# Expert numbers in a product-key retrieval: comparisons and products in float16, choices innermost, on VectorE

## The chip, the cores and the metric

The kernel runs on one core of a Trainium2 chip. The core has TensorE (PE, matrix products; PEld is its loading of weights), VectorE (DVE), ScalarE (ACT), GpSimd (POOL) and SyncE (SP, which here issues DMAs). The metric is the device time of one execution in microseconds (us); the time quoted is the median of several executions. Beside them stands one execution taken with the profiler, from which all rows below come.

## The reference

A decoder block for 512 tokens of 1024 channels: RMS norm, a mixer (RWKV-7 heads and sliding-window attention), an output product, and a channel mixer `peer_ffn` that fetches experts. Only the last is touched. Cut to what matters:

```python
def block(x_b):                                   # 128 tokens; H = 8 heads, K = 16
    q = (x_b @ wq).reshape(-1, H, 2, PEER_HALF)
    s = jnp.einsum('thcd,hcnd->thcn', q, subkeys)         # 128 scores for each half c
    s_top, i_top = lax.top_k(s, K)
    cand_s = (s_top[:, :, 0, :, None] + s_top[:, :, 1, None, :]).reshape(-1, H, K * K)
    cand_i = (i_top[:, :, 0, :, None] * PEER_N_KEYS + i_top[:, :, 1, None, :]).reshape(-1, H, K * K)
    best_s, best_pos = lax.top_k(cand_s, K)
    idx = jnp.take_along_axis(cand_i, best_pos, axis=-1).reshape(-1, H * K)
    gate = jax.nn.softmax(best_s, axis=-1).reshape(-1, H * K)
    u = u_tab[idx]
    act = jax.nn.gelu(jnp.einsum('td,ted->te', x_b, u), approximate=False)
    return jnp.einsum('te,ted->td', gate * act, v_tab[idx])
```

So for each token and head the 16 best keys of either half are found, their sums are ranked again, and the 16 winners give 16 expert numbers (first key x 128 + second key) with gates.

## The kernel before

Stages, in the time of the profiled execution: the mixer and the output product up to about 390 us; the choice of experts from there to about 600 us, which is where the change lies; a stage of one-hot products that lays the gates out over all experts (605 to about 820 us); and then products of all 128 blocks of experts with `u` and `v` on TensorE to the end. One token tile of the four goes through gathered rows instead (`gather`, on POOL's DMA queue).

**The choice.** The loop over `hc` (16 steps: 8 heads x 2 halves) splits a block of `wq` into high and low part (`wq_split`: `wqh` cast on ScalarE L165, `wql` subtracted on POOL L166), makes the query with 24 matmuls (`pq`), and the scores with four (`psc`, copied to `sc`). `top` (L926) then picks the 16 best of 128 scores on VectorE for the four token tiles: two MAX8, two index searches and one replacement per row, L929 to L937. After every four steps two heads are complete, which makes eight rows of 16 + 16 keys, `tv` values and `ti` numbers.

`choose(h0, tv, ti)` (L939) works on such a group of two heads. It is a generator that is advanced twice in each later step of the loop, so that a group's work lies among the next four steps; the last group (`h0` = 6) runs behind the loop. Up to the first stop: `fi`, the key numbers as float32; `df`, the differences of neighbouring numbers (L945, and an addition for the first half L946); and `cand`, the 50 sums that can be among the best 16 (nine instructions L951 and L953). `E_` is POOL for the first three groups and VectorE for the last. Then `top` on the candidates gives `bv` and `bp`, the positions 0 to 49. `ex` (L966) is the exponent's argument; ScalarE takes its exponential (L969 for the last group, L1005 otherwise).

`pick` (L976) turns positions into numbers without a gather. For each position it compares with 15 thresholds (`ge`, L981, four rows at once: 4 x 16 x 15 = 960 elements, two instructions, on VectorE), multiplies the 0/1 result with the differences (L987, two instructions, on `E_`), and sums (L992) and adds the first number (L993, VectorE). The first `pick` gives first key and place in the list (`offs` holds the thresholds, packed with the number by 128s), the second the second key (thresholds `iota`). Results go to `sg_`, the table of gates and key numbers that all later stages read.

**What runs beside it.** TensorE fills the time with products of `uT` blocks that belong to the later expert stage (`up_steps`, L896). For each of a list of 64 blocks: `up_load` on SyncE (four buffers `u`), `up_split` (`uh` cast on ScalarE L165; `ul` subtracted, L166, on POOL for block numbers 1 to 19 and on VectorE otherwise; two buffers each), `up_product` (24 matmuls of 384 columns in two steps, lines L175 to L177 in turn, each `ul` read by L177), and `up_act` (gelu on ScalarE, L888). The split of the next block is issued one block ahead. `UPS1` and `UPST` say how many half products follow each `hc` step (0, 1, 0, 0, then 2 each) and each stop of the last group (3 each). P14, P16, P17 and P18 in the text are products number 14, 16, 17 and 18 of that list, counted from 0.

The order on every engine is that in which the code is written (`manual_schedule`), the generators' interleaving included; an engine runs its list strictly in that order and waits at the front of it. All buffers of `choose` exist twice.

Of the kernel before, what the change touches and what calls it, by code (L numbers as in the profile page):

```python
# [7 lines left out]
F32 = mybir.dt.float32  # L8
F32R = mybir.dt.float32r
HF = mybir.dt.float16  # L10
# [3 lines left out]
OP = mybir.AluOpType  # L14
AX = mybir.AxisListType
# [7 lines left out]
TOPK = 16  # L23
# [31 lines left out]
OFFS = [sum(NCAND[:a]) for a in range(16)]  # L55
# [20 lines left out]
def _emit(ctx, tc, A, out, dbg, stop):  # L76
    nc = tc.nc
    V, SC, PE, GP, SY = nc.vector, nc.scalar, nc.tensor, nc.gpsimd, nc.sync
# [56 lines left out]
    for lv in range(5):  # L135
        b = 1 << lv
        n = 32 // (2 * b)
        for q in range(4):
# [5 lines left out]
                             pattern=[[-2 * b, n], [0, b]], compare_op=OP.is_ge, fill=0.0,  # L144
                             base=0, channel_multiplier=1)
# [621 lines left out]
    mpst, mp = right("mp")  # L767
# [3 lines left out]
    SY.dma_start(ln2r, A["ln2r"])  # L771
    iota = mp.tile([128, 128], F32, name="iota")
    GP.iota(iota, pattern=[[1, 128]], base=0, channel_multiplier=0, allow_small_or_imprecise_dtypes=True)

# [144 lines left out]

    offs = tk.tile([128, 2, 15], F32, name="offs")  # L920
    for a in range(1, 16):
        GP.memset(offs[:, 0, a - 1:a], float(OFFS[a]))
        GP.memset(offs[:, 1, a - 1:a], 128.0 * (OFFS[a] - OFFS[a - 1]))
    B815 = [128, 4, TOPK, 15]

# [13 lines left out]
    def choose(h0, tv, ti):  # L939

        E_ = GP if h0 < 6 else V
        fi = tk.tile([128, 2, 8, TOPK], F32, name="fi", tag="fi", bufs=2)
        V.tensor_copy(fi, ti)
        df = tk.tile([128, 2, 8, 15], F32, name="df", tag="df", bufs=2)
        E_.tensor_tensor(out=df, in0=fi[:, :, :, 1:16], in1=fi[:, :, :, 0:15], op=OP.subtract)  # L945
        E_.tensor_tensor(out=df[:, 0], in0=df[:, 0], in1=offs[:, 1, None, :].to_broadcast([128, 8, 15]), op=OP.add)  # L946
        cand = tk.tile([128, 8, NC_], F32, name="cand", tag="cand", bufs=2)
# [20 lines left out]
        if h0 == 6:  # L968
            SC.activation(ex, ex, AF.Exp)  # L969
        pf = tk.tile([128, 8, TOPK], F32, name="pf", tag="pf", bufs=2)  # L970
        V.tensor_copy(pf, bp)
        ro = tk.tile([128, 8, TOPK], F32, name="ro", tag="ro", bufs=2)
        rn = tk.tile([128, 8, TOPK], U32, name="rn", tag="rn", bufs=2)

        def pick(src, steps, base, dst):

            ges = []
            for hh in range(2):
                hs = slice(4 * hh, 4 * hh + 4)
                ge = tk.tile(B815, F32, name="ge", tag="ge", bufs=2)  # L980
                V.tensor_tensor(out=ge, in0=src[:, hs, :, None].to_broadcast(B815),  # L981
                                in1=steps[:, None, None, :].to_broadcast(B815), op=OP.is_ge)
                ges.append(ge)
            yield
            for hh in range(2):
                hs = slice(4 * hh, 4 * hh + 4)
                E_.tensor_tensor(out=ges[hh], in0=ges[hh],  # L987
                                                    in1=df[:, base, hs, None, :].to_broadcast(B815), op=OP.mult)
            yield
            for hh in range(2):  # L990
                hs = slice(4 * hh, 4 * hh + 4)
                V.tensor_reduce(dst(hh), ges[hh], axis=AX.X, op=OP.add)  # L992
                V.tensor_tensor(out=dst(hh), in0=dst(hh), in1=fi[:, base, hs, 0:1].to_broadcast([128, 4, TOPK]),  # L993
                                op=OP.add)


        yield from pick(pf, offs[:, 0, :], 0, lambda hh: ro[:, 4 * hh:4 * hh + 4])
        V.tensor_copy(bp, ro)
# [3 lines left out]
        V.tensor_tensor(out=pf, in0=pf, in1=ro, op=OP.subtract)  # L1002
        yield from pick(pf, iota[:, 1:16], 1, lambda hh: sg_[:, 2, :, h0 + hh, :])
        if h0 < 6:
# [394 lines left out]
```

## Time and profile before

| | us |
|---|---|
| median of 3 runs | 1654.14 |
| lowest, highest | 1652.88, 1655.71 |
| profiled execution, its time | 1651.63 |
| its span in the trace | 1649.9 |
| TensorE busy, of the span | 1584.4 (96%) |
| VectorE busy | 1279.5 (78%) |
| POOL busy | 712.3 (43%) |
| ScalarE busy | 655.2 (40%) |

The mean granted clock of TensorE is 0.992 of full speed. Busy shares are averages over stages that have different limits, so for the change only the stretch of the choice counts, about 430 to 600 us, and what waits there. In that stretch TensorE has matmuls to do nearly all the time, VectorE is full too, and POOL serves both: TensorE with `wql` and `ul`, VectorE with candidates and the products L987. The last chain of the page runs mostly over TensorE (49%), then VectorE (11%).

In rows of the timeline the first number is the start, the second the duration; in brackets stands how long the engine was idle before it and what released it.

### The profile page before, as it was taken

Reading aid. Unit: us, or ns where it says so; the run is one execution under the profiler, and the core shown is the slowest. Engines: PE = TensorE matmul, PEld = TensorE weight load, DVE = VectorE, ACT = ScalarE, POOL = GpSimd, SP = SyncE. Lnnn points to the kernel's source line nnn. Section 1 sums busy time; section 2 is a strip of 40 time slices with the busy share of each in tenths; the row PEclk is TensorE's granted clock in tenths of the full one; section 3 lists DMA queues with packets and bytes.
Section 4 is the critical chain, followed back from the end, with each engine's and each line's share of the span. In section 5 each row is a group of like instructions: output and inputs, shape, how many; then the busy total and the mean of one; then the engine's idle time right before and its main releaser. Section 6 shows DMA issues by size and latency. Waiting matters only on the chain.

```text
span 1649.9 us, 30181 instructions
## 1 busy us (share of the span) xinstructions
PE 1584.4 (96%) x11629; PEld 1362.9 (83%) x11629; DVE 1279.5 (78%) x2474; ACT 655.2 (40%) x1078; POOL 712.3 (43%) x670
## 2 busy tenths in 40 slices
PE   5999999898999989999999999999999999999997
PEld 4777677676898889888888888888888888888886
DVE  5656548745799989999868778877878877787797
ACT  5444345534343435445433333333333333333334
POOL 5112110033577612222235555555565655556582
PEclk9999999999999999999999999999999999999999
DMA  4111120141222249998999988988988989889794
GB/s 135 53 41 41 53 60 2 58 166 52 90 103 91 78 162 318 331 360 316 337 325 354 330 308 298 332 311 304 341 304 310 319 310 325 306 289 352 244 305 147
DMA packets 180113, 369.57 MB, mean 224 GB/s; under 512 B 17792, under 2 KB 102272, under 8 KB 179712
## 3 DMA queue, kind: packets, MB, share of 16 engines
q1 hardware_dynamic: 137056, 225.14, 40.0%
q0 software_dynamic: 36864, 134.23, 22.4%
q10 hardware_dynamic: 6048, 8.26, 1.4%
q8 instruction: 91, 1.49, 0.4%
q14 instruction: 54, 0.44, 0.1%
HBM read 332.04 MB, written 35.52 MB: 223 GB/s over the span
## 4 chain that ended last, share of the span: by engine, by line
PE 49%; DVE 11%; DMA 3%; issue 2%; ACT 1%; SPq 0%; POOL 0%; DVEq 0%; POOLq 0%; ACTq 0%
PE acc L1271 10%; PE acc L1269 10%; PE acc L1270 10%; PE pA L177 7%; PE pA L175 7%; PE pA L176 7%; DVE O L1140 3%; DVE ul L166 2%; DVE scr L1094 2%; DVE P L1145 2%; DMA u<-in_uT_dram 1%; DMA row<-in_vB_dram,ix 0%; DMA gts<-gates 0%; DMA acts<-actd 0%; PE pG L1167 0%
## 5 line engine op out<-in xcount | busy, mean ns | idle before, releaser
L177 PE MATMUL pA<-h2hi,ul 128*128 128x384 f32 x1024 | 348.3, 340 | 10.2 <-DVE ul L166 6.1
L175 PE MATMUL pA<-h2hi,uh 128*128 128x384 f32 x1024 | 354.0, 346 | 3.0 <-ACT uh L165 1.6
L176 PE MATMUL pA<-h2lo,uh 128*128 128x384 f32 x1024 | 346.4, 338 | 0.0
L1271 PE MATMUL acc<-vl,wh 128*128 128x512 f32 x768 | 299.1, 389 | 1.1 <-DVE vl L166 1.1
L1269 PE MATMUL acc<-vh,wh 128*128 128x512 f32 x768 | 299.5, 390 | 0.6 <-ACT vh L165 0.6
L1270 PE MATMUL acc<-vh,wl 128*128 128x512 f32 x768 | 299.3, 390 | 0.0
L1081 POOL DMA_INDIRECT row<-in_u_dram,ix x128 | 175.6, 1372 | 284.8 <-DVE scr L1094 246.5
L1081 POOL DMA_INDIRECT row<-in_vB_dram,ix x128 | 195.9, 1530 | 142.5 <-DVE x L1092 118.9
L166 DVE TENSOR_TENSOR vl<-v,vh 128x1024 fp32r<-128x1024 f32 x128 | 217.1, 1697 | 35.9 <-ACT vh L165 35.0
L177 PEld LDWEIGHTS pA<-h2hi,ul 128*128 128x128 f32 x1024 | 193.3, 189 | 15.3 <-DVE ul L166 11.2
L175 PEld LDWEIGHTS pA<-h2hi,uh 128*128 128x128 f32 x1024 | 193.4, 189 | 6.8 <-ACT uh L165 2.1
L176 PEld LDWEIGHTS pA<-h2lo,uh 128*128 128x128 f32 x1024 | 193.4, 189 | 3.0
L1092 DVE SCALAR_TENSOR_TENSOR x<-row,ac,x 128x1024 f32<-128x1024 f32 x128 | 172.6, 1348 | 6.0 <-DMA row<-in_vB_dram,ix 4.2
L1271 PEld LDWEIGHTS acc<-vl,wh 128*128 128x128 f32 x768 | 144.2, 188 | 32.6 <-DVE vl L166 2.1
L1269 PEld LDWEIGHTS acc<-vh,wh 128*128 128x128 f32 x768 | 144.2, 188 | 28.5 <-ACT vh L165 0.9
L1270 PEld LDWEIGHTS acc<-vh,wl 128*128 128x128 f32 x768 | 144.1, 188 | 27.4
L1094 DVE SCALAR_TENSOR_TENSOR scr<-row,h2g 128x1024 f32<-128x1024 f32 x128 | 158.8, 1240 | 1.5 <-DMA row<-in_u_dram,ix 0.2
L165 ACT CAST uh<-u 128x1024 fp32r<-128x1024 f32 x128 | 133.9, 1047 | 61.3 <-PE pA L176 33.0
L166 DVE TENSOR_TENSOR ul<-u,uh 128x1024 fp32r<-128x1024 f32 x109 | 134.8, 1238 | 21.2 <-ACT uh L165 20.9
L165 ACT CAST vh<-v 128x1024 fp32r<-128x1024 f32 x128 | 134.0, 1047 | 0.1
L1168 ACT ACTIVATE gst<-pG 128x512 f32<-128x512 f32 x96 | 55.9, 597 | 100.6 <-PE pG L1167 98.8
L888 ACT ACTIVATE act<-pA 128x384 f32<-128x384 f32 x86 | 42.2, 491 | 132.6 <-PE pA L177 132.6
(711 smaller groups left out, 2508.0 us busy)
## 6 DMA issues: line engine op xcount, KB each, us to landing
u<-in_uT_dram SPq DMA_DIRECT2D x128, 512.0 KB, 8.1
v<-in_vB_dram SPq DMA_DIRECT2D x128, 512.0 KB, 6.3
gts<-gates SPq DMA_DIRECT2D x384, 64.0 KB, 5.1
gates<-gst SPq DMA_DIRECT2D x11, 2048.0 KB, 11.8
w<-in_w_in_dram SPq DMA_DIRECT2D x40, 256.0 KB, 3.2
wq<-in_wq_dram SPq DMA_DIRECT2D x16, 512.0 KB, 3.5
acts<-actd ACTq DMA_DIRECT2D x42, 192.0 KB, 6.1
act<-acts SPq DMA_DIRECT2D x42, 192.0 KB
```

What stands on the lines that cost most here:

```text
L165: (hi_eng or SC.copy)(dst_hi, src)
L166: (lo_eng or V).tensor_tensor(out=dst_lo, in0=src, in1=dst_hi.bitcast(F32), op=OP.subtract)
L175: mm(ps, whi[k][:, :m], ahi[:, k], start=k == 0, stop=False)
L176: mm(ps, whi[k][:, :m], alo[:, k], start=False, stop=False)
L177: mm(ps, wlo[k][:, :m], ahi[:, k], start=False, stop=k == KD - 1)
L1081: GP.indirect_dma_start(r_, None, A["vB"].rearrange("b p d -> (b p) d") if w_ else A["u"], bass.IndirectOffsetOnAxis(ap=ix[:, w_, jj:jj + ...
L1092: V.scalar_tensor_tensor(x2[:, 0, :], r_, ac[:, jj:jj + 1], x2[:, 0, :], op0=OP.mult, op1=OP.add)
L1094: V.scalar_tensor_tensor(scr, r_, 1.0, h2g, op0=OP.mult, op1=OP.mult, accum_out=ac[:, jj:jj + 1])
L1168: SC.activation(gst[:, :, :, t4 * 4:t4 * 4 + 4].rearrange("p n g t -> p (n g) t"), p.rearrange("p t e -> p e t"), AF.Copy, scale=1.0 / GS)
L1269: mm(o, wh[:, ts], vh[:, ds_], start=b == 0, stop=False)
L1270: mm(o, wl[:, ts], vh[:, ds_], start=False, stop=False)
L1271: mm(o, wh[:, ts], vl[:, ds_], start=False, stop=b == 127)
```

## The change

The key numbers `fi` and the places `pf` become float16. The thresholds become tables `stepA` (17 steps) and `stepB` (16 steps) of float16 with the 16 choices innermost, in place of `offs` and `iota`. The first number is a step of its own whose threshold is always reached, so it is summed with the others. In `stepA` the second threshold stands twice, and the 2048 that the place in the list needs there is added as 1024 in each of the two steps. The differences `dA` and `dB` carry each value twice in a row, and are made by six instructions on `E_` in place of two. `ge` has the order row, step, choice; the products are written as pairs; both products of `pick` are VectorE's in all groups; the sum reads the steps with a stride. The addition behind the sum is gone. Cut to its core:

```diff
-    iota = mp.tile([128, 128], F32, name="iota")
-    GP.iota(iota, pattern=[[1, 128]], base=0, channel_multiplier=0, allow_small_or_imprecise_dtypes=True)
...
-    offs = tk.tile([128, 2, 15], F32, name="offs")
-    for a in range(1, 16):
-        GP.memset(offs[:, 0, a - 1:a], float(OFFS[a]))
-        GP.memset(offs[:, 1, a - 1:a], 128.0 * (OFFS[a] - OFFS[a - 1]))
-    B815 = [128, 4, TOPK, 15]
+    KA, KB = TOPK + 1, TOPK
+    stepA = tk.tile([128, KA, TOPK], HF, name="stepA")
+    stepB = tk.tile([128, KB, TOPK], HF, name="stepB")
+    addA = tk.tile([128, KA, 2], HF, name="addA")
+    for k in range(KA):
+        a = max(k - 1, 0)
+        GP.memset(stepA[:, k], float((0, OFFS[1], OFFS[a])[min(k, 2)]))
+        GP.memset(addA[:, k], 0.0 if k == 0 else 1024.0 if k < 3 else 128.0 * (OFFS[a] - OFFS[a - 1]))
+        if k < KB:
+            GP.memset(stepB[:, k], float(k))
...
         E_ = GP if h0 < 6 else V
-        fi = tk.tile([128, 2, 8, TOPK], F32, name="fi", tag="fi", bufs=2)
+        fi = tk.tile([128, 2, 8, TOPK], HF, name="fi", tag="fi", bufs=2)
         V.tensor_copy(fi, ti)
-        df = tk.tile([128, 2, 8, 15], F32, name="df", tag="df", bufs=2)
-        E_.tensor_tensor(out=df, in0=fi[:, :, :, 1:16], in1=fi[:, :, :, 0:15], op=OP.subtract)
-        E_.tensor_tensor(out=df[:, 0], in0=df[:, 0], in1=offs[:, 1, None, :].to_broadcast([128, 8, 15]), op=OP.add)
+        dA = tk.tile([128, 8, KA, 2], HF, name="dA", tag="dA", bufs=2)
+        dB = tk.tile([128, 8, KB, 2], HF, name="dB", tag="dB", bufs=2)
+        for half, d, n in ((0, dA, 2), (1, dB, 1)):
+            if n == 2:
+                E_.memset(d[:, :, 1], 0.0)
+            E_.tensor_copy(d[:, :, 0], fi[:, half, :, 0:1].to_broadcast([128, 8, 2]))
+            E_.tensor_tensor(out=d[:, :, n:], in0=fi[:, half, :, 1:16, None].to_broadcast([128, 8, 15, 2]),
+                             in1=fi[:, half, :, 0:15, None].to_broadcast([128, 8, 15, 2]), op=OP.subtract)
+        E_.tensor_tensor(out=dA, in0=dA, in1=addA[:, None].to_broadcast([128, 8, KA, 2]), op=OP.add)
...
-                ge = tk.tile(B815, F32, name="ge", tag="ge", bufs=2)
-                V.tensor_tensor(out=ge, in0=src[:, hs, :, None].to_broadcast(B815),
-                                in1=steps[:, None, None, :].to_broadcast(B815), op=OP.is_ge)
+                ge = tk.tile([128, 4, KA, TOPK], HF, name="ge", tag="ge", bufs=2)[:, :, 0:K]
+                V.tensor_tensor(out=ge, in0=pf[:, hs, None, :].to_broadcast([128, 4, K, TOPK]),
+                                in1=steps[:, None].to_broadcast([128, 4, K, TOPK]), op=OP.is_ge)
...
-                E_.tensor_tensor(out=ges[hh], in0=ges[hh],
-                                                    in1=df[:, base, hs, None, :].to_broadcast(B815), op=OP.mult)
+                pairs = ges[hh].rearrange("p g k (s t) -> p g k s t", t=2)
+                V.tensor_tensor(out=pairs, in0=pairs,
+                                in1=d[:, hs, :, None, :].to_broadcast([128, 4, K, TOPK // 2, 2]), op=OP.mult)
...
-                V.tensor_reduce(dst(hh), ges[hh], axis=AX.X, op=OP.add)
-                V.tensor_tensor(out=dst(hh), in0=dst(hh), in1=fi[:, base, hs, 0:1].to_broadcast([128, 4, TOPK]),
-                                op=OP.add)
+                V.tensor_reduce(dst(hh), ges[hh].rearrange("p g k s -> p g s k"), axis=AX.X, op=OP.add)
```

On POOL, at the end of the `hc` loop, the list before reads as follows (`wql` and `ul` are the low parts of the splits; L953 is the last candidate instruction of the third group; a number behind an x counts instructions in a row):

```order
L953 TENSOR_TENSOR cand<-tv 128x8x8
L166 TENSOR_TENSOR wql<-wq,wqh 128x1024
L166 TENSOR_TENSOR ul<-u,uh 128x1024
L166 TENSOR_TENSOR wql<-wq,wqh 128x1024
L166 TENSOR_TENSOR ul<-u,uh 128x1024
L987 TENSOR_TENSOR ge<-ge,df 128x960 x2
L166 TENSOR_TENSOR ul<-u,uh 128x1024
L987 TENSOR_TENSOR ge<-ge,df 128x960 x2
L166 TENSOR_TENSOR ul<-u,uh 128x1024 x6
```

The same place with the change:

```order
L964 TENSOR_TENSOR cand<-tv 128x8x8
L166 TENSOR_TENSOR wql<-wq,wqh 128x1024
L166 TENSOR_TENSOR ul<-u,uh 128x1024
L166 TENSOR_TENSOR wql<-wq,wqh 128x1024
L166 TENSOR_TENSOR ul<-u,uh 128x1024 x8
```

The four products are no longer in POOL's list, and every `ul` there now directly follows the one ahead of it.

On VectorE, at the start of the last group, before:

```order
L943 CAST fi<-ti 128x256
L945 TENSOR_TENSOR df<-fi 128x240
L946 TENSOR_TENSOR df<-df,offs 128x120
L951 TENSOR_TENSOR cand<-tv 128x8x16
L951 TENSOR_TENSOR cand<-tv 128x8x8
```

And with the change:

```order
L947 CAST fi<-ti 128x256
L953 MEMSET dA 128x8
L954 COPY dA<-fi 128x8x2
L955 TENSOR_TENSOR dA<-fi 128x8x30
L954 COPY dB<-fi 128x8x2
L955 TENSOR_TENSOR dB<-fi 128x8x30
L957 TENSOR_TENSOR dA<-dA,addA 128x272
L962 TENSOR_TENSOR cand<-tv 128x8x16
L962 TENSOR_TENSOR cand<-tv 128x8x8
```

Between the cast and the first candidates there are six instructions where two stood. In each `pick` VectorE's list now holds two comparisons, then two products, and later two sums without additions. The lists of TensorE, ScalarE and SyncE are the same before and after.

## Rows read from the trace of the kernel before

**Rows 1.** Windows: from:to, length, busy us (instructions) of PE, PEld, DVE, ACT, POOL, clock, DMA, GB/s

```profile
557.65:562.65 5.00, 5.00 (x16) 5.00 (x17) 4.83 (x18) 0.00 (x0) 2.27 (x1) 0.50 0.60 197
640.00:680.00 40.00, 37.34 (x300) 34.32 (x296) 38.95 (x60) 20.57 (x37) 9.38 (x8) 1.00 0.97 340
1000.00:1040.00 40.00, 40.00 (x199) 35.97 (x199) 33.20 (x41) 13.62 (x19) 22.07 (x17) 1.00 0.87 313
```

**Rows 2.** Timeline of VectorE, 538 to 601 us: start, duration, line, operation, out<-in

```profile
538.98 0.86 DVE L929 MAX8 tv<-sc 128x8 f32<-128x128 f32 x4
...
543.67 1.13 DVE L992 TENSOR_REDUCE ro<-ge 128x64 f32<-128x960 f32 x1
...
546.16 1.62 DVE L993 TENSOR_TENSOR ro<-ro,fi 128x64 f32<-128x64 f32 x1
...
560.82 0.28 DVE L943 CAST fi<-ti 128x256 f32<-128x256 uint32 x1
...
561.78 0.98 DVE L951 TENSOR_TENSOR cand<-tv 128x128 f32<-128x128 f32 x8
...
562.93 0.55 DVE L929 MAX8 bv<-cand 128x8 f32<-128x50 f32 x4
...
569.05 0.28 DVE L966 TENSOR_TENSOR ex<-bv 128x128 f32<-128x128 f32 x1
...
600.10 0.29 DVE L1017 TENSOR_TENSOR sg__4943<-ex,gs 128x128 f32<-128x128 f32 x1
```

**Rows 3.** Waits of TensorE, 530 to 640 us: total us, times, longest

```profile
PE pA L177 <- POOL ul L166: 3.7, 1, 3.7
...
PE pA L177 <- DVE ul L166: 0.8, 1, 0.8
```

**Rows 4.** Timeline of TensorE, from 562.87 us

```profile
562.87 0.34 PE L175 MATMUL pA<-h2hi,uh 128*128 128x384 f32 x1
563.05 0.33 PE L176 MATMUL pA<-h2lo,uh 128*128 128x384 f32 x1
```

**Rows 5.** Timeline of POOL: copies of an early stage, and 545 to 560 us

```profile
174.91 2.59 POOL L487 COPY TF<-TT 32x256 f32<-32x256 f32 x4 [0.18 <-DVE TT L479]
...
545.30 2.39 POOL L166 TENSOR_TENSOR ul<-u,uh 128x1024 fp32r<-128x1024 f32 x1 [2.23 <-ACT uh L165]
550.36 4.93 POOL L987 TENSOR_TENSOR ge<-ge,df 128x960 f32<-128x960 f32 x2 [2.66 <-DVE ge L981]
555.25 4.67 POOL L166 TENSOR_TENSOR ul<-u,uh 128x1024 fp32r<-128x1024 f32 x2
```

**Rows 6.** Timeline of ScalarE, 549 to 582 us

```profile
549.47 1.04 ACT L165 CAST uh<-u 128x1024 fp32r<-128x1024 f32 x1
...
570.96 0.31 ACT L969 ACTIVATE ex<-ex 128x128 f32<-128x128 f32 x1
572.44 1.05 ACT L165 CAST uh<-u 128x1024 fp32r<-128x1024 f32 x1 [1.16 <-POOL ul L166]
...
580.89 1.05 ACT L165 CAST uh<-u 128x1024 fp32r<-128x1024 f32 x1 [2.79 <-POOL ul L166]
```

**Rows 7.** Timeline of VectorE: a comparison of `pick`, and a one-hot comparison in float16

```profile
537.91 1.14 DVE L981 TENSOR_TENSOR ge<-pf,offs 128x960 f32<-128x960 f32 x1
...
605.09 0.69 DVE L1140 TENSOR_TENSOR O<-iota,sK 128x1024 f16<-128x1024 f16 x1
```

**Rows 8.** All of line L365: ns least/median/most, first and last start

```profile
L365 DVE TENSOR_SCALAR B<-B x4: 415/422/622, 57.6 to 175.8; 128x512 f32<-128x512 f32 x4
```

**Rows 9.** Timelines: POOL's only float16 work; POOL from 475 us; TensorE at 483 us

```profile
308.06 1.52 POOL L776 IOTA iota<- 128x256 f16 x1
...
475.73 0.59 POOL L945 TENSOR_TENSOR df<-fi 128x240 f32<-128x240 f32 x1 [1.26 <-DVE fi L943]
...
478.88 2.41 POOL L166 TENSOR_TENSOR wql<-wq,wqh 128x1024 fp32r<-128x1024 f32 x1
...
483.34 0.39 PE L177 MATMUL pq<-h2hi,wql 128*128 128x512 f32 x1
```

More of the change, by code (lines that the diff above doesn't have):

```diff
@@ L969, in choose @@
             SC.activation(ex, ex, AF.Exp)
-        pf = tk.tile([128, 8, TOPK], F32, name="pf", tag="pf", bufs=2)
+        pf = tk.tile([128, 8, TOPK], HF, name="pf", tag="pf", bufs=2)
         V.tensor_copy(pf, bp)
@@ L973, in choose, with pick @@
         rn = tk.tile([128, 8, TOPK], U32, name="rn", tag="rn", bufs=2)
-        def pick(src, steps, base, dst):
+        def pick(steps, d, K, dst):
             ges = []
@@ L986, in pick @@
                 hs = slice(4 * hh, 4 * hh + 4)
-                E_.tensor_tensor(out=ges[hh], in0=ges[hh],
-                                                    in1=df[:, base, hs, None, :].to_broadcast(B815), op=OP.mult)
+                pairs = ges[hh].rearrange("p g k (s t) -> p g k s t", t=2)
+                V.tensor_tensor(out=pairs, in0=pairs,
+                                in1=d[:, hs, :, None, :].to_broadcast([128, 4, K, TOPK // 2, 2]), op=OP.mult)
             yield
             for hh in range(2):
-                hs = slice(4 * hh, 4 * hh + 4)
-                V.tensor_reduce(dst(hh), ges[hh], axis=AX.X, op=OP.add)
-                V.tensor_tensor(out=dst(hh), in0=dst(hh), in1=fi[:, base, hs, 0:1].to_broadcast([128, 4, TOPK]),
-                                op=OP.add)
-        yield from pick(pf, offs[:, 0, :], 0, lambda hh: ro[:, 4 * hh:4 * hh + 4])
+                V.tensor_reduce(dst(hh), ges[hh].rearrange("p g k s -> p g s k"), axis=AX.X, op=OP.add)
+        yield from pick(stepA, dA, KA, lambda hh: ro[:, 4 * hh:4 * hh + 4])
         V.tensor_copy(bp, ro)
@@ L1002, in choose @@
         V.tensor_tensor(out=pf, in0=pf, in1=ro, op=OP.subtract)
-        yield from pick(pf, iota[:, 1:16], 1, lambda hh: sg_[:, 2, :, h0 + hh, :])
+        yield from pick(stepB, dB, KB, lambda hh: sg_[:, 2, :, h0 + hh, :])
         if h0 < 6:
```

## Prediction

> **What bounds the kernel now.** I read the page first, then the stages by windows, then the waits of TensorE, and last the stretch from 534 to 601 us engine by engine. From about 900 us on TensorE has no idle time: 40.00 of 40 us at 1000 [rows 1]. From about 605 to 820 us VectorE is the full engine, 38.95 of 40 us, with the one-hot work [rows 1]. Neither stage is edited, and both begin when the last `sg_` is written, at 600.10 + 0.29 = 600.39 us [rows 2]. So the question is by how much that moment moves; later work only shifts with it.
>
> From 530 us on TensorE runs without a gap until 554 us. Then it waits 3.7 us for one `ul` on POOL and later 0.8 us for one on DVE [rows 3]. The first wait is POOL's own doing: two products `ge*df` stand ahead of that `ul` from 550.36, for 4.93 us, and the `ul` follows at 555.25 [rows 5]. I call the product that waits P14 (the up product 14 of the list) and count on: P18 is the one whose `uh` is cast at 572.44. After the wait TensorE is not at once at full speed. [...] That costs (5.0 - 16 x 0.175) = 2.2 us more. Wait and half clock together are about 6 us.
>
> **The change part by part.** *Products leave POOL.* Without the two at 550.36, the `ul` of P14 can start as soon as its `uh` is cast, 549.47 + 1.04 = 550.51 [rows 6], and ends at about 553, before TensorE asks for it at 554. The 6 us are gone there, and TensorE would come to P18 at about 570.7 instead of 576.7. That is the whole possible gain; what is late next decides how much stays.
>
> *What VectorE does for a pick.* Two 32-bit comparisons at 1.15 [rows 7] become two comparisons and two products in 16 bits. No row shows these; the nearest is the one-hot instruction, 1024 elements of float16 in 0.69 us [rows 7], which has the same pair-wise broadcast. I take 0.61 to 0.69 each, 2.5 to 2.7 us for four. The two reductions grow from 960 to 1088 elements or 1024, and no row has a float16 input with a stride; bounds are half of 1.13 [rows 2] and 1.13 x 1088/960 = 1.28; I take 1.2, nearest to the row. The two additions behind them go. Their price is almost all waiting: the one at 546.16 took 1.62 us and ended as POOL's `ul` of 545.30 + 2.39 did [rows 2, 5]. An instruction of VectorE with two inputs in SBUF stands still while POOL runs a TENSOR_TENSOR. This is the rule that decides here.
>
> [...] I take casts as held; what it would be otherwise stands below.
>
> *The ledger of VectorE to the last candidates.* The reductions of the last overlapped pick start at 543.67 before [rows 2], now at about 544.1 (four instructions for two, behind the same wait). Two of 1.2 end at 546.5. The cast behind them is held by the `ul` of 545.30 until 547.6, and with five small ones (1.25 us in the same place before) the second comparisons start at 548.8. Three 16-bit instructions are through at 550.65; there POOL takes its turn with P14's `ul`, and the fourth waits until 553.0 and ends at 553.6. The top-16 of the last scores takes 4.7 us (538.98 to 543.67 [rows 2]) and ends at 558.3. Reductions end at 560.6. The `ul` of P16, cast at P14's new end, 557.7, is on POOL from 558.85 to 561.25 and holds the casts: `fi` is ready at 562.3, before at 561.10 [rows 2]. In the last group VectorE itself then makes `dA` and `dB`, six instructions instead of two, 1.2 us (bounds 0.7, what the two took from 561.10 to 561.78 [rows 2], and 1.8), and the candidates, 1.15 as from 561.78 to 562.93. The `ul` of P17 on POOL from 563.05 to 565.45 falls right among them. Candidates end at 567.1; from there to `ex` are 6.4 us as before (562.93 to 569.33 [rows 2]): `ex` at 573.5 instead of 569.33.
>
> *Who waits for that.* ScalarE's exponential of `ex` stands ahead of P18's `uh` in its queue. Before, it ran at 570.96 and `uh` at 572.44, when P16 let go of the buffer [rows 6]: 1.2 us of slack. Now `uh` starts at 573.85, takes 1.05, `ul` on POOL 2.4, and TensorE resumes P18 at 577.4 after some 6.7 us of idle time. So the wait of P14 is back at P18, longer, and the half clock (2.2 us) with it: P18 ends at 583.6, before at 580.89 [rows 6], 2.7 us late. From there on TensorE sets the pace in both kernels. The later 0.8 us wait goes, since VectorE is early, and the reductions without additions behind the last `ul` give back 0.5: the last `sg_` is 1.4 us late.
>
> *The middle groups.* There POOL makes `dA` and `dB`, in two groups with a `wql` close behind, the first at 475.73 us. Before, `df` is two instructions, the first of 0.59 us, the second, half its size, by estimate 0.4; the `wql` ends at 478.88 + 2.41 = 481.29, and TensorE uses it at 483.34 [rows 9]: 2.05 us of cover. Six instructions by the price of the first row (two of 240 at 0.59, one of 272 at 0.65, a copy at 0.25 twice, a memset at 0.1) are 2.4 us, so 1.4 more, and `fi` comes 0.5 later: the cover falls to 0.15. I put 0.1 us on it. The 20 more memsets on POOL at 390 lie in a wait of POOL for ScalarE, and the removed iota at 308 frees nobody: both nothing.
>
> *Sum.* 1.4 + 0.1 = +1.5 us on the profiled execution's 1651.63 (span 1649.9 and 1.7 around it), 1653.1. The median of the runs shown is 2.5 above that execution, so I forecast 1655.5.
>
> [...]
>
> **The rivals.** *Faster: VectorE slips through between two splits.* Casts not held put the second comparisons at 547.9, all four are through at 550.4, just before POOL's turn, `fi` is ready at 558.7, and the candidates have to fit between 561.1 and 563.05. With 1.2 + 1.15 us they don't quite, and `ex` at 572.4 gives +0.1 us (1654.3, still my forecast's case). If they do, `ex` is at 569.7, P18 resumes at 573.6 and ends at 579.8, 1.1 early; with the later gains 2.4 us less, 1651.7; without a half clock 4.6 less, 1649.5; and with no hold at all 6.6 less, 1647.5. For it: the misses are a tenth of a us to half of one. Against it: the ledger misses both times. Centre 1650.5, chance 0.18.
>
> *Slower: POOL's six small instructions.* POOL has one float16 row, the iota at 1.52 us for 256 elements [rows 9]; a 240-element subtraction in 32 bits takes 0.59. Were the three TENSOR_TENSORs 1.5 each, the six would take 5.1 us, the `wql` would be 2.5 us late for TensorE in each of two groups: +5.0, 1660.5. It decides once the six take more than 2.6 us. Against it: an iota is another kind of work. Chance 0.15.
>
> *Slower: the change doesn't do what it says.* If the comparisons don't run at the double rate, four take 4.7 us, they meet two splits each, and `ex` is some 7 us later still: about 1663. Against it stands the 0.69 us row [rows 7]; chance 0.05.
>
> **How the numbers follow.** My forecast, with `ex` between 572.4 and 573.9, has 0.62 and runs from 1654 to 1657. About 0.2% (3.3 us, 1650.8 to 1657.5) is what a measurement of this kernel can tell from no change. Forecast: 0.53 inside, 0.07 above, 0.02 below, since the runs shown spread by 1.5 us to either side. First rival: 0.15 below, 0.03 inside. POOL rival: 0.14 above, 0.01 inside. Rate rival: 0.05 above. That makes 0.17 faster, 0.57 same, 0.26 slower. The range 1650.0 to 1660.0 leaves out the lower part of the first rival (0.07), the upper part of the second (0.06) and the third (0.05).
>
> **What would show it.** Right: no wait of P14's matmuls at 554; a TensorE gap of 5 us or more near 571 to 577, ended by a POOL `ul`, with half clock behind it; candidates on VectorE stretched by 2 us or more; `ex` on ScalarE after 572. Wrong: `ex` before 570 and `sg_` before 598 (first rival); waits of TensorE for `wql` at 483 and 526 (second); comparisons above 1 us without a POOL instruction beside them (third). A last `sg_` later or earlier without the end following would break the shift argument.

## The result, and the profile after

| | before | after |
|---|---|---|
| median | 1653.51 | 1667.61 |
| lowest, highest | 1649.79, 1655.71 | 1665.19, 1668.28 |
| span of the profiled execution | 1649.9 | 1666.1 |

Times in us, four executions each. The ratio of after to before is 1.0083, with a 95% interval from 1.0065 to 1.0102: the change costs 14 us. I had forecast 1655.5 with a range up to 1660.0; it came out 7.6 us above the upper end.

The stages behind the choice are what they were. The windows of after (from:to, length, busy us and instructions of PE, PEld, DVE, ACT, POOL, granted clock, DMA share, GB/s), the last two some 16 us later in the program than in [rows 1]:

```profile
588.20:593.20 5.00, 5.00 (x16) 4.84 (x17) 4.01 (x2) 1.27 (x2) 3.07 (x2) 0.50 0.38 129
656.00:696.00 40.00, 37.41 (x289) 34.23 (x287) 38.94 (x59) 18.70 (x34) 9.38 (x8) 0.96 0.96 341
1016.00:1056.00 40.00, 40.00 (x200) 35.97 (x199) 33.78 (x40) 13.62 (x19) 22.00 (x17) 1.00 0.88 315
```

VectorE is full in the one-hot stage (38.94 of 40) and TensorE in the last one (40.00 of 40), as before. The stretch at half clock (0.50, 16 matmuls in 5 us) now lies at 588, behind the wait for P18, no longer at 557. What moved is the end of the choice. VectorE's timeline of after, the lines that answer to [rows 2]:

```profile
554.53 4.46 DVE L1003 TENSOR_REDUCE ro<-ge 128x64 f32<-128x1088 f16 x2
...
576.20 0.28 DVE L947 CAST fi<-ti 128x256 f16<-128x256 uint32 x1
...
577.53 0.98 DVE L962 TENSOR_TENSOR cand<-tv 128x128 f32<-128x128 f32 x8
...
584.80 0.27 DVE L977 TENSOR_TENSOR ex<-bv 128x128 f32<-128x128 f32 x1
...
616.72 0.29 DVE L1026 TENSOR_TENSOR sg__4941<-ex,gs 128x128 f32<-128x128 f32 x1
```

The last `sg_` ends at 617.01 where it ended at 600.39, 16.6 us later, and the span is 16.2 us longer. Some 3 us of that are no part of the change: the first `fi` of after stands at 427.34, that of before at 424.30, and in the kernels of the experiments, which hardly differ ahead of it, it lies anywhere between 424.2 and 427.2. I therefore count from the first `fi`. Before, it is 176.1 us from there to the last `sg_`, after, 189.7: 13.6 us more, about as much as the medians differ (14.1).

The prices of `pick` on VectorE in after (each line of the code: least, median and greatest ns of one, first and last start, shape):

```profile
L992 DVE TENSOR_TENSOR ge<-pf,stepA x8: 711/721/2784, 452.1 to 585.9; 128x1088 f16<-128x1088 f16 x8
L992 DVE TENSOR_TENSOR ge<-pf,stepB x8: 684/692/2889, 471.4 to 604.0; 128x1024 f16<-128x1024 f16 x8
L999 DVE TENSOR_TENSOR ge<-ge,dA x8: 710/1795/2919, 455.5 to 589.3; 128x1088 f16<-128x1088 f16 x8
L999 DVE TENSOR_TENSOR ge<-ge,dB x8: 676/684/2898, 472.6 to 607.4; 128x1024 f16<-128x1024 f16 x8
L1003 DVE TENSOR_REDUCE ro<-ge x8: 2190/2288/2358, 463.6 to 599.8; 128x64 f32<-128x1088 f16 x8
L1003 DVE TENSOR_REDUCE sg__4941<-ge x8: 1968/2148/2261, 478.5 to 614.2; 128x64 f32<-128x1024 f16 x8
```

Comparisons and products take the 0.7 us that I had put on them, where nothing stands in their way. The sums do not: 2.29 and 2.15 us at the median, and none below 1.97, where I had put 1.2 and had called 1.28 the upper bound. Sixteen sums at some 1 us too much are about the size of the loss.

Where TensorE feels it is in its waits of after, 400 to 640 us (total us, times, longest):

```profile
PE pA L175 <- ACT act L886: 7.8, 1, 7.8
PE pq L177 <- POOL wql L166: 5.0, 2, 3.9
...
PE pA L177 <- DVE ul L166: 2.3, 2, 1.6
```

The 3.7 us for the `ul` of P14 are gone [rows 3]. In their place stand two waits for `wql`, in the middle groups, and one wait of 7.8 us, which is P18's. The first `wql` wait, followed back over POOL and TensorE (timeline: start, duration, idle time before it and what ended that):

```profile
483.89 0.20 POOL L954 COPY dA<-fi 128x16 f16<-128x16 f16 x1 [7.66 <-DVE fi L947]
...
487.97 2.34 POOL L166 TENSOR_TENSOR wql<-wq,wqh 128x1024 fp32r<-128x1024 f32 x1
...
490.37 0.51 PE L177 MATMUL pq<-h2hi,wql 128*128 128x512 f32 x1 [3.89 <-POOL wql L166]
```

POOL stood idle for 7.66 us, waiting for `fi`; its own six small instructions and the candidates then took 4.1 us, and TensorE waited for the `wql` behind them. So it is VectorE that comes late with `fi`. The P18 wait, over ScalarE and TensorE:

```profile
585.10 0.31 ACT L980 ACTIVATE ex<-ex 128x128 f32<-128x128 f32 x1 [10.47 <-DVE ex L977]
585.32 1.03 ACT L165 CAST uh<-u 128x1024 fp32r<-128x1024 f32 x1
...
588.20 0.69 PE L175 MATMUL pA<-h2hi,uh 128*128 128x384 f32 x1 [7.79 <-ACT act L886]
```

ScalarE sat for 10.47 us in front of the exponential, with the `uh` of P18 behind it in its queue, as the prediction described it, only longer. What came last for TensorE, by the bracket of 588.20, was the gelu `act` that stands behind that `uh` on ScalarE, and not the `ul` on POOL that I had named.

### The profile page after: what moved, and what is told of

It is laid out like the page before. It is cut to its first block, busy times and chain, and to the rows that moved or that the text cites. A ratio compares the mean times of both kernels' runs of the same rounds, so it can differ in the third digit from the quotient of the medians.

```text
span 1666.1 us, 30193 instructions
## 1 busy us (share of the span) xinstructions
PE 1590.6 (95%) x11629; PEld 1368.7 (82%) x11629; DVE 1292.4 (78%) x2474; ACT 654.6 (39%) x1078; POOL 684.0 (41%) x689
## 4 chain that ended last, share of the span: by engine, by line
PE 51%; DVE 10%; issue 1%; DMA 1%; ACT 1%; SPq 0%; DVEq 0%
PE acc L1278 10%; PE acc L1280 10%; PE acc L1279 10%; PE pA L175 7%; PE pA L177 6%; PE pA L176 6%; DVE O L1149 3%; DVE ul L166 2%; DVE scr L1103 2%; DVE P L1154 2%; PE pG L1176 1%; DMA acts<-actd 0%; DMA u<-in_uT_dram 0%; DMA v<-in_vB_dram 0%; SPq L1217 0%
## 5 line engine op out<-in xcount | busy, mean ns | idle before, releaser
L886 ACT ACTIVATE act<-pA 128x384 f32<-128x384 f32 x86 | 42.2, 491 | 132.9 <-PE pA L177 132.8
```

## The experiments

The theory at the start (stride): a sum that reads its values 32 bytes apart takes twice as long as one that reads them side by side; all of the missed time follows from that. Rivals: the float16 input is slow (type); the products on VectorE are what costs (load).

To compare kernels stage by stage I use one table, from the timelines of VectorE: us from the first `fi` to the second, third and fourth, and from the fourth to the end of the last `sg_`.

| kernel | 1 to 2 | 2 to 3 | 3 to 4 | 4 to `sg_` | sum | ratio of times to before |
|---|---|---|---|---|---|---|
| before | 51.1 | 42.9 | 42.6 | 39.6 | 176.1 | |
| after | 56.2 | 45.7 | 47.0 | 40.8 | 189.7 | 1.0083 |
| e1 | 52.9 | 43.5 | 42.2 | 38.1 | 176.7 | 1.0015 [1.0002, 1.0028] |
| e2 | 54.4 | 44.3 | 44.2 | 41.3 | 184.2 | 1.0056 [1.0036, 1.0076] |
| e3 | 49.8 | 42.7 | 42.6 | 40.8 | 175.9 | 0.9999 [0.9987, 1.0011] |
| e4 | 56.2 | 45.6 | 47.0 | 36.0 | 184.8 | 1.0068 [1.0047, 1.0090] |
| e5 | 53.3 | 44.1 | 46.3 | 35.7 | 179.3 | 1.0025 [1.0014, 1.0036] |
| e6 | 53.3 | 44.1 | 46.3 | 30.2 | 173.8 | 0.9987 [0.9978, 0.9997] |
| e8, its fastest execution | 50.1 | 42.8 | 45.0 | 41.4 | 179.3 | 1.0053 [1.0034, 1.0072] |
| e8 again | 52.3 | 45.6 | 43.7 | 41.2 | 182.8 | (one time, 1664.2) |
| e9 | 52.9 | 43.5 | 42.2 | 32.1 | 170.7 | 0.9979 [0.9966, 0.9991] |
| e12 | 54.4 | 45.7 | 43.5 | 34.4 | 178.0 | 1.0015 [0.9999, 1.0031] |

For after, e3 and e6 this sum differs from that of before by within 1 us of what the medians do. In the other kernels it does not hold the whole effect: their times are 1.6 to 3.0 us worse than the sum says (4.2 and 5.5 in the two profiles of e8). Something is lost behind the last `sg_`, where I had said that later work only shifts. From the last `sg_` to the end of the span there are 1049.5 us before and 1049.1 after, but 1052.8 in e1 and 1055.5 in e9. The first and the eighteenth matmul of `acc` behind the one-hot stage, in before and then in e9:

```profile
841.90 0.50 PE L1269 MATMUL acc<-vh,wh 128*128 128x512 f32 x1 [0.56 <-ACT vh L165]
...
847.00 0.39 PE L1271 MATMUL acc<-vl,wh 128*128 128x512 f32 x1
```

```profile
840.16 0.50 PE L1278 MATMUL acc<-vh,wh 128*128 128x512 f32 x1 [1.84 <-ACT vh L165]
...
848.07 0.39 PE L1280 MATMUL acc<-vl,wh 128*128 128x512 f32 x1
```

At the last `sg_` e9 is 4.2 us ahead of before, at the first of these 1.7, at the eighteenth 1.1 behind: TensorE waits longer for a `vh`, and the granted clock behind that wait is 0.50 in the 5 us from 842.4, where before it is 1.00 in the 5 us from 843.8. The span of that execution of e9 is 1.8 us longer than that of before, although its median is lower. So an earlier `sg_` need not arrive in the time.

**e1: steps innermost.** The edit of after, at its core:

```diff
-        V.tensor_copy(pf, bp)
+        V.tensor_copy(pf, bp[:, :, :, None].to_broadcast([128, 8, TOPK, 2]))
...
-                V.tensor_tensor(out=ge, in0=pf[:, hs, None, :].to_broadcast([128, 4, K, TOPK]),
-                                in1=steps[:, None].to_broadcast([128, 4, K, TOPK]), op=OP.is_ge)
+                V.tensor_tensor(out=ge.rearrange("p (r k t) -> p r k t", r=64, t=2),
+                                in0=pf[:, hs].rearrange("p g s t -> p (g s) t")[:, :, None, :].to_broadcast([128, 64, K // 2, 2]),
+                                in1=steps.rearrange("p (k t) -> p k t", t=2)[:, None].to_broadcast([128, 64, K // 2, 2]), op=OP.is_ge)
...
-                V.tensor_reduce(dst(hh), ges[hh].rearrange("p g k s -> p g s k"), axis=AX.X, op=OP.add)
+                V.tensor_reduce(dst(hh), ges[hh].rearrange("p (g s k) -> p g s k", g=4, s=TOPK), axis=AX.X, op=OP.add)
```

> Kernel after, but with the steps innermost: float16, all on VectorE and the first number as a step of its own stay, each place stands twice in a row so that comparisons keep their pairs, the first list is filled up to 18 steps, and the sum reads its 18 or 16 values side by side. Theory stride (the sum is slow because it reads its values 32 bytes apart): sums fall from 2.29 and 2.15 us to about 1.35 and 1.2, comparisons and products stay near 0.7, the wait for P18 falls from 7.8 to below 5 us, time 1652 to 1657. Rival type (a float16 input makes the sum slow): sums stay at 2.1 to 2.4 us and the time at 1665 to 1670. Rival load (the products on VectorE cost the time, whatever the sums do): sums fall, time stays above 1662.

Measured: 1655.89 us median of ten, before on the same chip 1652.49. The sums of e1, and TensorE's waits, 400 to 640 us:

```profile
L1006 DVE TENSOR_REDUCE ro<-ge x8: 1327/1340/1347, 461.8 to 587.3; 128x64 f32<-128x1152 f16 x8
L1006 DVE TENSOR_REDUCE sg__4941<-ge x8: 1195/1206/1212, 475.1 to 599.9; 128x64 f32<-128x1024 f16 x8
```

```profile
PE pA L175 <- ACT act L886: 5.3, 1, 5.3
...
PE pq L177 <- POOL wql L166: 0.4, 1, 0.4
```

The sums are at 1.34 and 1.21 us with the same float16 input. Type falls; the order of the values in memory is what counts for the price of the sum. The wait for P18 is 5.3 us and not below 5, a near miss, while the time is where stride put it. With the sums near the price that I had assumed, the kernel also ends where I had forecast: 1655.9 for 1655.5, the last `sg_` at 602.00 for 601.8, P18 resumed at 577.68 for 577.4.

Part of that agreement is luck. The first `fi` of e1 is 1.0 us later than that of before, which is no part of the change. Counted from it, the fourth `fi` comes 2.0 us later than before, where the ledger had 1.2, and the last group is 1.4 us shorter, where the ledger had it 0.2 longer: 0.6 in all for 1.4. More of e1's time is lost behind the last `sg_`, 3.3 us between the profiled executions. e1 also differs from after in more than the order: its differences carry no twin, so POOL's small instructions behind `fi` take 1.4 us for 2.0. They are not what shortens the first interval, since e8 below keeps them as in after and has it at 50.1 and 52.3 us.

**e2: the choices innermost alone, in the kernel before.**

```diff
-    B815 = [128, 4, TOPK, 15]
+    B815 = [128, 4, 15, TOPK]
...
-                V.tensor_reduce(dst(hh), ges[hh], axis=AX.X, op=OP.add)
+                V.tensor_reduce(dst(hh), ges[hh].rearrange("p g k s -> p g s k"), axis=AX.X, op=OP.add)
```

> Kernel before with one part of the change alone: `ge` in the order row, step, choice, still float32, products on POOL, additions kept; the sum reads with a stride of 64 bytes. Stride: sums rise from 1.14 to about 2.1 us, comparisons stay near 1.15, time 1662 to 1670. Type: sums stay at 1.14 and the time at 1653.

Measured: 1662.6 us. The sums of e2:

```profile
L992 DVE TENSOR_REDUCE ro<-ge x8: 1841/1850/1861, 459.1 to 590.2; 128x64 f32<-128x960 f32 x8
L992 DVE TENSOR_REDUCE sg__4943<-ge x8: 1750/1814/1839, 473.4 to 606.8; 128x64 f32<-128x960 f32 x8
```

The time is at the lower end of what stride gave. The sums take 1.8 us for 960 values, less than the 2.1 I expected but far from 1.14. With float32 and 64 bytes between the values the sum slows down as well, and the kernel before loses 10 us by that one edit.

**e3: the products of the first three groups back on POOL.**

```diff
-                V.tensor_tensor(out=pairs, in0=pairs,
+                E_.tensor_tensor(out=pairs, in0=pairs,
```

> Kernel after with the products of the first three groups back on POOL, as before, in float16. Stride: sums stay at 2.2 us; VectorE is rid of 12 products of 0.7 us, POOL has 12 of 2 to 2.5 us again, TensorE waits for a `ul` behind them once more, and the time is between 1660 and 1672. Rival load: the time returns to 1652 to 1657.

Measured: 1652.89 us, the time of before. A wait of TensorE and the products of e3 on POOL:

```profile
PE pA L177 <- POOL ul L166: 2.2, 1, 2.2
```

```profile
L999 POOL TENSOR_TENSOR ge<-ge,dA x6: 2041/2220/2400, 454.3 to 542.2; 128x1088 f16<-128x1088 f16 x6
L999 POOL TENSOR_TENSOR ge<-ge,dB x6: 1929/2092/2256, 466.2 to 554.0; 128x1024 f16<-128x1024 f16 x6
```

Here the time is the one that load gave and not the one that stride gave, although the sums stay at 2.29 and 2.13 us. So neither is the whole cause. Undoing the slow sums alone gives back 11.7 us (1667.6 to 1655.9), undoing the move of the products alone 14.7, and the loss as a whole is only 14.1. The two shares cannot be added: both load VectorE within a group, and there TensorE does not notice up to a limit. With either of them undone the second `fi` comes no later than 52.9 us behind the first, and the wait for `wql` is 0.4 us or nothing; with both in place it is 56.2 and TensorE waits 5.0 in all. The other kernels fit that: 2.0 us of waits for `wql` at 53.3 (e5), 13.4 at 59.3 (e10).

**e4: the exponential of the last group behind its second pick.**

```diff
-        if h0 == 6:
-            SC.activation(ex, ex, AF.Exp)
...
-        if h0 < 6:
-            SC.activation(ex, ex, AF.Exp)
+        SC.activation(ex, ex, AF.Exp)
```

> Kernel after with the exponential of the last group issued behind its second pick, as in the other groups, so that it no longer stands ahead of the `uh` of P18 on ScalarE. Theory queue (P18's wait is the exponential waiting for `ex`): the 7.8 us wait at 580 to 588 goes, with its half clock, and TensorE is some 10 us earlier there; the last `sg_` comes 5 to 10 us earlier than 617, time 1657 to 1662. Rival VectorE-bound (VectorE has no idle time up to the last `sg_`): the wait goes, but the last `sg_` stays within 2 us of 617 and the time within 1665 to 1668.

Measured: 1664.16 us, 3.5 less than after; the intervals of the two ratios overlap (1.0047 to 1.0090, and 1.0065 to 1.0102), so the size of that gain is not certain. TensorE's waits of e4:

```profile
PE pA L177 <- DVE ul L166: 6.4, 3, 3.7
PE pq L177 <- POOL wql L166: 4.9, 2, 3.9
```

The 7.8 us are gone, so it was the exponential that held P18. The last group shrinks from 40.8 to 36.0 us, the lower end of what queue expected, and the time misses its 1657 to 1662: a large part comes back as waits of TensorE for a `ul` of VectorE, 6.4 us for 2.3, which is the next that is late. The middle groups stay as slow as in after, as they must.

**e9: steps innermost, with the exponential behind** (the edits of e1 and e4 together).

> Steps innermost, and the exponential of the last group behind its second pick. With the steps innermost alone TensorE still waits 5.3 us for P18, with some 2 us of half clock. Theory queue: that wait goes, and since VectorE then has only short waits left, the last `sg_` comes 2 to 5 us earlier than 602, time 1649 to 1653. Rival VectorE-bound: the wait comes back at a later `ul` of VectorE, the last `sg_` within 1 us of 602, time 1654 to 1657.

Measured: 1651.33 us, before 1655.03, ratio 0.9979 [0.9966, 0.9991]: faster than before, if only by 0.2%. The waits of TensorE in e9, the largest one ahead of the last `sg_` and that for `wql`:

```profile
PE pA L177 <- DVE ul L166: 1.8, 2, 1.1
...
PE pq L177 <- POOL wql L166: 0.4, 1, 0.4
```

The last group takes 32.1 us, where e1 has 38.1. Queue holds: the wait is gone and the time is in its range; the last `sg_`, at 596.18, is 5.8 us earlier than 602, a little more than the 2 to 5 expected.

**e5 and e6: the sum by halving additions**, over all eight rows at once, choices innermost as in after; e6 with the edit of e4 added. The core for a second pick (the first one adds its upper levels in float32):

```diff
-            for hh in range(2):
-                V.tensor_reduce(dst(hh), ges[hh].rearrange("p g k s -> p g s k"), axis=AX.X, op=OP.add)
+            V.tensor_tensor(out=all_[:, :, K - 16:K - 8], in0=all_[:, :, K - 16:K - 8], in1=all_[:, :, K - 8:K], op=OP.add)
+            if K == KB:
+                for n in (4, 2):
+                    V.tensor_tensor(out=all_[:, :, 0:n], in0=all_[:, :, 0:n], in1=all_[:, :, n:2 * n], op=OP.add)
...
```

> Kernel after with choices innermost as they are, but the sum by halving additions over all eight rows at once: in the second pick four additions in float16, in the first one in float16 and four with float32 sums. By the prices of this case a second pick's sum takes about 1.4 us for eight rows where two reductions take 4.2, a first pick's about 2.0 where they take 4.5. Unlike a reduction an addition has two inputs in SBUF and stands still beside POOL's work. Theory stride: time 1650 to 1656, the wait for P18 below 5 us. Rival hold (each sum meets a TENSOR_TENSOR of POOL and loses up to 2.4 us there): time 1657 to 1664.

> Halving additions, and the exponential of the last group behind its second pick. Queue: no wait for P18, time 3 to 6 us below that of the halving additions alone, 1646 to 1652. VectorE-bound: no more than 1 us below it.

Measured: 1659.78 for e5, 1653.57 for e6, before 1655.03. The first additions of e5, and a second pick's sum that nothing disturbs:

```profile
L1003 DVE TENSOR_TENSOR ge<-ge x8: 671/684/2048, 461.6 to 601.9; 128x1024 f16<-128x1024 f16 x8
```

```profile
475.98 0.68 DVE L1003 TENSOR_TENSOR ge<-ge 128x1024 f16<-128x1024 f16 x1
476.69 0.75 DVE L1006 TENSOR_TENSOR ge<-ge 128x512 f16<-128x512 f16 x2
477.47 0.29 DVE L1007 TENSOR_TENSOR sg__4941<-ge 128x128 f32<-128x128 f16 x1
```

Undisturbed it is through in 1.8 us, where two reductions of e1 take 2.3. But some stand still beside POOL (2.05 us for 0.68), and in all VectorE spends 21.8 us on these additions, 19.7 on the sums of e1; the wait for P18 is 7.1 us. So e5 is where hold put it, and no better than e1. e6 has no P18 wait and gains 6.2 us on e5, a little more than queue gave, though its time misses the 1646 to 1652 with its starting point.

**e8, e11, e10: how far apart may the values lie.** After, with the choices in pairs (e8), fours (e11) and eights (e10), so that a sum reads its steps 4, 8 and 16 bytes apart. The core of e8:

```diff
+                ge = tk.tile([128, 64 * KA], HF, name="ge", tag="ge", bufs=2)[:, 0:64 * K].rearrange("p (r k t) -> p r k t", r=32, t=2)
+                V.tensor_tensor(out=ge, in0=pf[:, hs].rearrange("p g (s t) -> p (g s) t", t=2)[:, :, None, :].to_broadcast([128, 32, K, 2]),
+                                in1=steps[:, None, :, 0:2].to_broadcast([128, 32, K, 2]), op=OP.is_ge)
```

> Kernel after with the choices in pairs: `ge` in the order row, pair of choices, step, choice within the pair, so that the sum reads its steps 4 bytes apart where it read them 32 bytes apart; comparisons, products and their counts as in after. Theory any stride (neighbouring values must be side by side): sums stay at 2.0 to 2.3 us and the time at 1664 to 1668. Rival long stride (only steps far apart cost): sums fall to 1.2 to 1.4 us and the time to 1653 to 1657, as with the steps innermost.

> The same with the choices in fours, 8 bytes apart, products in four times as many instructions. Threshold: 1.15 to 1.25 us for 1024 values. Gradual: 1.25 to 1.5.

> Kernel after with the choices in eights, so that the sum reads its steps 16 bytes apart; to look at the price of the sum alone (the products are cut in twice as many instructions and read each difference without its twin, so the time says little). So far: 2 bytes 1.20, 4 bytes 1.16, 32 bytes 2.15 us for 1024 values of float16. Theory threshold (free as long as neighbouring reads are close): 1.15 to 1.25 here, and the price jumps between 16 and 32 bytes. Theory gradual (price grows with the distance): 1.5 to 1.9.

The sums of the second picks, 1024 values each, of e8, e11 and e10, one fence for each kernel:

```profile
L1003 DVE TENSOR_REDUCE sg__4941<-ge x8: 1193/1206/1224, 473.1 to 603.3; 128x64 f32<-128x1024 f16 x8
```

```profile
L1005 DVE TENSOR_REDUCE sg__4941<-ge x8: 1196/1205/1212, 481.7 to 612.5; 128x64 f32<-128x1024 f16 x8
```

```profile
L1005 DVE TENSOR_REDUCE sg__4941<-ge x8: 1933/2000/2009, 480.7 to 623.2; 128x64 f32<-128x1024 f16 x8
```

At 2 (e1), 4 and 8 bytes the sum costs the same 1.21 us (the 1.16 at 4 bytes in the expectation of e10 is not in the row); at 16 bytes 2.00, at 32 bytes (after) 2.15. e10 and e11 are one execution each, with eight such sums. "Any stride" falls, and so does "gradual". Threshold was right that there is a jump, and wrong about its place, which is between 8 and 16 bytes. Why it lies there no run shows.

The times of e10 and e11, 1680.0 and 1670.3, are those of kernels with more and slower products and say nothing of the sums. That of e8 says something that I had not expected: 1663.66 median, from 1658.14 to 1671.6, though its sums are those of e1. One reason stands in its comparisons:

```profile
L992 DVE TENSOR_TENSOR ge<-pf,stepB x8: 1176/1191/1208, 465.0 to 593.6; 128x1024 f16<-128x1024 f16 x8
```

1.19 us for 0.69 in after. They read the thresholds as pairs that lie 32 bytes apart, out of a table made for sixteen, and each pair of places again for every step. It is the thresholds that cost: e1 repeats its pairs of places too, with the thresholds side by side, and takes 0.69, and so does e11, which reads fours 32 bytes apart. Sixteen comparisons at half a microsecond more are 8 us of VectorE, which takes back half of what the sums gave.

**e8 again**, for the width of its times.

> Choices in pairs once more, for a second profile of one of its executions: the first one profiled was the fastest of eight. If this one is above 1661, its trace shows where the 3 us or more lie: theory queue, a longer wait for P18; rival hold, more comparisons or products above 2 us ahead of `wql` or `ul` waits of TensorE.

Measured: 1664.2 us. POOL and VectorE in the second group, first in the execution at 1658.1, then in the one at 1664.2:

```profile
493.29 0.28 DVE L977 TENSOR_TENSOR ex<-bv 128x128 f32<-128x128 f32 x1
...
493.56 2.38 POOL L166 TENSOR_TENSOR ul<-u,uh 128x1024 fp32r<-128x1024 f32 x1 [4.61 <-ACT uh L165]
```

```profile
493.13 2.38 POOL L166 TENSOR_TENSOR ul<-u,uh 128x1024 fp32r<-128x1024 f32 x1 [3.85 <-ACT uh L165]
...
493.41 2.25 DVE L977 TENSOR_TENSOR ex<-bv 128x128 f32<-128x128 f32 x1
...
509.09 2.46 POOL L166 TENSOR_TENSOR wql<-wq,wqh 128x1024 fp32r<-128x1024 f32 x1 [2.88 <-ACT wqh L165]
...
509.33 2.31 DVE L1009 TENSOR_SCALAR bp<-bp 128x128 uint32<-128x128 uint32 x1
...
523.37 0.28 DVE L947 CAST fi<-ti 128x256 f16<-128x256 uint32 x1
...
530.20 0.78 PE L177 MATMUL pq<-h2hi,wql 128*128 128x512 f32 x1 [2.56 <-POOL wql L166]
```

In the first, the subtraction for `ex` starts 0.27 us ahead of POOL's `ul` and takes 0.28. In the second it starts 0.28 us behind it and takes 2.25; a TENSOR_SCALAR is then caught by the next `wql` in the same way, `fi` stands at 523.37 for 519.06, and TensorE waits 2.56 us for a `wql` where it did not wait. Its wait for P18 is shorter, 5.1 for 6.0. So in this execution the loss that lies in the choice is hold, 3.5 us by the table; another 2.5 of the 6.1 between the two times lie elsewhere. A shift of half a microsecond decided which instructions of VectorE met one of POOL. Whether every slower execution of e8 loses its time there was not traced.

**e12: pairs, with the exponential behind.**

> Choices in pairs, and the exponential of the last group behind its second pick. Pairs alone were profiled at 1658.1 us, but their other executions went up to 1671.6, while steps innermost alone gave 1655.9 with the same sums. Theory queue (what is lost hangs on the wait for P18): the wait goes, time 1649 to 1655 and a narrow spread. Rival hold (comparisons and products caught by POOL's `ul` anywhere, which a shift of a few tenths of a us decides): the spread stays and the median is above 1656.

Measured: 1657.47 us, 1651.81 to 1663.25. The wait for P18 is gone and the spread stays, with two waits for `wql` of 4.7 us together in the profiled execution, which is the slowest of the ten: hold is what this fits, and the faster executions were not traced.

## Why the prediction was wrong

**The step that failed** is one term of VectorE's ledger: "I take 1.2, nearest to the row", for a sum over float16 values with a stride, with bounds from half of 1.13 to 1.28 us. The row behind it [rows 2] is a sum that reads its values side by side. I had said that no row has a float16 input with a stride and then bounded the type only; the stride got no bound of its own. Measured: 2.29 and 2.15. e1, which takes the stride away and leaves the type, gives 1.34 and 1.21.

**What the bounds left out.** The type, which they were about, costs nothing here: side by side the sum takes 1.21 us for 1024 float16 values (e1) and 1.14 for 960 float32 ones (before), 1.18 and 1.19 ns each. The distance between the values, which they did not cover, takes the 1.21 us to 2.15 (after).

**What the term did to the sum.** It did not come in as 16 x 1 us. The ledger followed VectorE through the end of the third group and the last one only. In the middle groups I had left a cover of 0.15 us, with `fi` taken as 0.5 later, and priced its loss at 0.1; with `fi` 5.1 us later behind the first group, TensorE waits 3.9 and 1.1 us for `wql`, with a mean granted clock of 0.68 in the 5 us from 490, and the three intervals from one `fi` to the next cost 5.1 + 2.8 + 4.4 = 12.3 us of the 13.6, where the ledger had 1.2 in the third of them. The last group is only 1.2 us longer. That the slow sums alone do not cost the time, but only together with the products that came to VectorE, is what e3 shows. The addition of 1653.1 and 2.5 was also a tenth short; it makes 1655.6.

**What held.** P14's wait is gone, and P18's has taken its place, caused by the exponential in ScalarE's queue, with the half clock behind it: 7.8 us where 6.7 were forecast, and 5.3 with the sums near my price. That 7.8 lies so near to 6.7 is luck. The 2.2 us of half clock behind it rest on [rows 1] and [rows 4], and after shows the same 16 matmuls in the 5.00 us from 588.20, 0.32 us apart at a granted clock of 0.50. One of the signs that I had given is missing in after: the candidates take 0.98 us there, as before, since `fi` at 576.20 comes after POOL's `ul` of 573.03 to 575.45 and meets none. In e1 they meet one and take 3.22 us. In after, `ex` is late because `fi` is. Comparisons and products: 0.61 to 0.69 forecast, 0.68 to 0.72 measured. Casts are held by POOL as I had assumed, and sums are not. In after, POOL's `wql` and `ul` and beside them VectorE:

```profile
467.93 2.40 POOL L166 TENSOR_TENSOR wql<-wq,wqh 128x1024 fp32r<-128x1024 f32 x1 [2.88 <-ACT wqh L165]
...
568.81 2.42 POOL L166 TENSOR_TENSOR ul<-u,uh 128x1024 fp32r<-128x1024 f32 x1 [1.55 <-ACT uh L165]
```

```profile
468.09 2.32 DVE L1007 CAST bp<-ro 128x128 uint32<-128x128 f32 x1
...
569.59 4.41 DVE L1003 TENSOR_REDUCE sg__4941<-ge 128x64 f32<-128x1024 f16 x2
```

A cast that takes 0.23 otherwise ends with the `wql`; the two sums take 2.2 each with the `ul` beside them, as everywhere. Of a hold without two inputs the rows of before had one sign, the greatest time of a TENSOR_SCALAR in [rows 8], beside POOL's copies in [rows 5]. Instructions with two inputs in SBUF were held as forecast: `ex` of after takes 2.25 us at 544.87, until POOL's `ul` of 544.59 to 546.97 is over, and 0.27 at 584.80. In before a subtraction with both inputs in SBUF, `wl` at 342.02, takes 2.49 us beside POOL's `wql` of 341.55 to 343.96, 0.69 at 172.61; an addition that reads one input from PSUM (`pj`, written by TensorE), `x2T` at 344.43, takes 0.68 beside an addition of POOL (343.92 to 345.66), 0.69 at the median. And in after the later stages only shift: 16.6 us at the last `sg_`, 16.2 at the end; in e1 and e9 they do not.

**The rivals.** POOL's six small instructions cost 0.1 to 0.66 us each, 2.4 in all, as estimated; a float16 TENSOR_TENSOR of 240 takes 0.59, no more than in 32 bits. The mark that I had given for that rival, waits for `wql`, is nevertheless in the trace, with another cause: POOL idle for `fi` ahead of them. The rate rival had a price near the result (1663) and the wrong operation: not the comparisons but the sums run at little more than half the rate. The faster rival is in no run that keeps the products on VectorE: even in e1 `ex` stands at 574.27, where that rival needed 569.7.

## What to carry to other kernels

Putting a dimension innermost to speed one instruction moves the stride to the next one that reads the data: price every reader of the new layout by a row that reads with its stride, and where there is none, bound the stride apart from the type. A cover of a few tenths of a microsecond is no cover: what came later than it made TensorE wait (3.9 us in after) and, here, run at a lower clock behind the wait (0.68 in the 5 us from 490). And look at what stands ahead of a needed copy in a queue: moving one small exponential was worth 6.2 us from e5 to e6, and some 3.5 in the kernel after, where the intervals overlap.

## What was new about the hardware

A VectorE sum of 1024 float16 values takes 1.21 us with 2, 4 or 8 bytes between neighbours (e1, e8, e11), 2.00 with 16 (e10) and 2.15 with 32 (after); of 960 float32 values 1.14 with 4 bytes (before) and 1.8 with 64 (e2). A float16 comparison that fetches its thresholds in pairs 32 bytes apart takes 1.19 us (e8) for 0.69 (after). The sums of after were not held by POOL's TENSOR_TENSOR (2.0 to 2.4 us throughout), while a cast (2.32 us for 0.23, in after), a TENSOR_SCALAR (2.31 for 0.23, in e8 again) and a two-input subtraction (2.25 for 0.28, in e8 again) took until POOL's instruction was over.
